# Scales for split weights: integer steps on VectorE in place of a maximum and a power on GpSimd

## The chip, the cores and the metric

The kernel runs on one core of a Trainium2 chip. The core has TensorE (PE in the profile), which multiplies matrices, VectorE (DVE), ScalarE (ACT), GpSimd (POOL), and SyncE (SP), which here only issues transfers. The engines run side by side, each with a queue of its own that it works off in order, and wait for one another through semaphores. The metric is the device time of one execution in microseconds (us). In the profile, times are counted from the first instruction, so its span is a little shorter than the execution.

## The reference

One encoder layer over 1024 tokens with 1024 features, in float32:

```python
hn = rmsnorm(x, norm_mix);  proj = hn @ w_in
o_a = window_gqa_sink(...)            # 8 heads, window 128, learned sink
o_b = neighbourhood_attention(...)    # 8 heads on the 16 x 64 grid
mix = concat([rmsnorm(o_a, norm_a), rmsnorm(o_b, norm_b)])
h = x + mix @ w_out
hn = rmsnorm(h, norm_ffn)
g, u = hn @ w_gate, hn @ w_up         # 2816 hidden columns
g = depthwise_conv3(g) + conv_b
h = h + (silu(g) * u) @ w_down
out = rmsnorm(h, norm_final)
```

## The kernel before, in words

**Products in parts.** Most float32 operands of PE are split: a high part (the value rounded to float16) and a low part (the rest). A product is then three matmuls, high by high, high by low and low by high. For float16 the operand is first brought to a good size by a scale that is a power of two, which is taken out again behind the product. ACT makes the high part (`activation` with `scale=`), DVE the low part (`scalar_tensor_tensor`: source times scale, minus the high part). In the feed-forward part this is `split_w` (L1140 and L1141) and `two_parts` (L1061 and L1062).

**Where a scale comes from.** For each block of 128 hidden columns ("unit"), ACT squares the block of `w_gate` and of `w_up` and sums each row (`head_scan`, L1054, for the first four units; `scan_rows`, L1154, for the others). The row sums stand in `head_rows` and `w_rows`. `settle_scales` takes them for up to four units at once. It adds the sums of gate and up (`wv`, L1021, on POOL) and calls `measure`. It then takes the reciprocal `back` (L1024, DVE), multiplies it by a common factor (L1025, POOL) and scales the three taps of the convolution of each unit by it (L1028, POOL).

**`measure`**, called with high priority, is a chain of steps on a tile of 128 by n numbers, n from 1 to 4:

- `spread_max`: PE transposes each column to all partitions (`wm`, L1001), DVE takes the maximum (L1003);
- L1010, POOL: the maximum with 1e-24, times 2^-26;
- L1011, POOL: the power -1/2;
- `exponent` (L240), DVE: a bit mask that keeps the exponent only, so that the scale is a power of two.

It runs ten times. Seven runs are from `settle_scales`: two with n = 2 in the second half of the output projection, four with n = 4 and one with n = 2 in the feed-forward part (`Weights.load`, L1277, for every fourth unit). Three are from `joint`, with n = 1: for `w_down` (L1598), and twice for the gated product (L1602 and L1715).

**The order of the work.** The input projection and the two attentions are interleaved. The output projection follows in two halves: `OutA` for the first four row blocks of `mix`, and the loop at L1233 to L1259 for the last four. This loop runs over two halves of the tokens (h) and eight output blocks (d). For each pair, PE runs 12 matmuls (L179) into a bank `pj`; DVE adds the result to `h1` (`settle_out`, L1188); ACT squares it (L1192), and the squares are summed on POOL for h = 0 (L1194) and on DVE for h = 1. `load_wo` splits the next block of `w_out` (ACT L1088, DVE L1089). Beside that the loop prepares the weights of the first four units: `settle_scales` at (h, d) = (0, 1) and (0, 3), `pure` and `head_weights` (ACT L1061, DVE L1062, and sums and differences of blocks, POOL L1209 and DVE L1201). When h = 0 is done, `inverse_power` gives the root mean square of the half: PE transposes (L220), DVE sums (L222, L223), POOL takes a power (L224). `widen` (PE, L255, tile `sw`) spreads it over the partitions, and DVE normalises `h1` with it (L1199).

The feed-forward part replaces eight block products of a 2 by 2 blocked product by seven (`p1` to `p7`, and `PRODUCTS` for the way down), with more sums and differences of blocks on DVE. A unit's results go to DRAM (`keep`) and come back as operands of the product with `w_down` (tile `dn`, `x_load`, `x_split`).

**What sets the order in the queues.** PE's instructions keep the order of the program (`manual_schedule`, L126). On the other engines the framework sorts the instructions when the program is built, by readiness and by priority: the place in the program, moved ahead inside a `high_priority` block. An instruction can thus run long before the program's place for it: the L1021 of the second group of feed-forward units ran at 472.31 us, its maximum (L1003) at 561.87 us. Buffers (14 tiles of the kind `op`, three `raw`, four each of `wv` and `m`) limit how far ahead that goes.

Of the kernel before, what the change touches and what calls it, by code (L numbers as in the profile page):

```python
# [16 lines left out]
I32 = mybir.dt.int32  # L17
AF = mybir.ActivationFunctionType
ALU = mybir.AluOpType
# [36 lines left out]
C_END = 128  # L56
V_TOP, P_TOP, TINY = 2.0 ** 14, 2.0 ** 15, 1e-30
X_TOP, W_TOP, FAINT = 2.0 ** 7, 2.0 ** 13, 1e-24

K_ID, K_MA, K_MB, K_SCALE, K_END = 0, 128, 512, 896, 897  # L60


def hybrid_layer(tc, xT, w_in, w_out, w_gate, w_up, w_down, small, sink, rpb, consts, rope, out):
    nc = tc.nc
    with ExitStack() as ctx:
# [25 lines left out]
        def bank(name, tag):  # L91
            return psum.tile([128, HALF], F32, name=name, tag=tag)
# [13 lines left out]
        minus_half = cpool.tile([128, 4], F32, name="minus_half")  # L106
# [109 lines left out]
        def inverse_power(sq, dim, tag):  # L216

            ps = bank("st", tag)
            for c in range(4):
                nc.tensor.transpose(ps[:, c * 128:(c + 1) * 128], sq[:, c * 128:(c + 1) * 128], ident)  # L220
            v = cpool.tile([128, 4], F32, name="v4", tag="v4", bufs=4)
            nc.vector.tensor_reduce(v, ps[:, :].rearrange("p (c w) -> p c w", w=128), axis=mybir.AxisListType.X, op=ALU.add)  # L222
            nc.vector.tensor_scalar(v, v, 1.0 / dim, EPS, op0=ALU.mult, op1=ALU.add)  # L223
            nc.gpsimd.tensor_tensor(v, v, minus_half, op=ALU.pow)  # L224
            return v

        def inverse_narrow(sqs, dim, tag, n=4):

            ps = bank("ss", tag)
            for i, sq in enumerate(sqs):  # L230
                for c in range(n):
                    nc.tensor.matmul(ps[:, c:c + 1], sq[:, c * 128:(c + 1) * 128], ones[:, 0:1], start=c == 0 and i == 0,
                                     stop=i == len(sqs) - 1, skip_group_check=True)
            v = cpool.tile([128, 4], F32, name="v4", tag="v4", bufs=4)
            nc.scalar.activation(v[:, 0:n], ps[:, 0:n], AF.Sqrt, bias=eps, scale=float(D) / dim)
            nc.vector.reciprocal(v[:, 0:n], v[:, 0:n])
            return v

        def exponent(x):
            nc.vector.tensor_scalar(x.bitcast(I32), x.bitcast(I32), 0x7F800000, None, op0=ALU.bitwise_and)  # L240
# [745 lines left out]
        def little(n, name, tag, bufs):  # L986

            if littles[1]:
                return littles[1].tile([128, n], F32, name=name, tag=tag, bufs=bufs)
            littles[0] += n  # L990
            return cst[:, littles[0] - n:littles[0]]

        def small(name, n=1):
            return little(n, name, name, 6)

        def spread_max(v, tag):

            n = v.shape[1]
            ps = bank("wm", tag)
            for i in range(n):  # L1000
                nc.tensor.transpose(ps[:, 128 * i:128 * i + 128], v[:, i:i + 1].to_broadcast([128, 128]), ident)  # L1001
            m = small("m", 4)[:, 0:n]
            nc.vector.tensor_reduce(m, ps[:, 0:128 * n].rearrange("p (c w) -> p c w", w=128), axis=mybir.AxisListType.X, op=ALU.max)  # L1003
            return m

        def measure(v, tag):

            with tc.high_priority(offset=500):
                s = spread_max(v, tag)
                nc.gpsimd.tensor_scalar(s, s, FAINT, W_TOP ** -2, op0=ALU.max, op1=ALU.mult)  # L1010
                nc.gpsimd.tensor_tensor(s, s, minus_half[:, 0:s.shape[1]], op=ALU.pow)  # L1011
                exponent(s)
            return s

        def settle_scales(i, n, tag):

            fs = FO[i:i + n]
            n = len(fs)
            rows = (w_rows if i >= HEAD else head_rows)[:, 2 * i:2 * i + 2 * n].rearrange("p (n s) -> p n s", s=2)
            v = small("wv", 4)[:, 0:n]  # L1020
            nc.gpsimd.tensor_tensor(v, rows[:, :, 0], rows[:, :, 1], op=ALU.add)  # L1021
            s = measure(v, tag)
            back = little(4, "back", "backs", 4)[:, 0:n]
            nc.vector.reciprocal(back, s)  # L1024
            nc.gpsimd.tensor_tensor(back, back, unit_back.to_broadcast([128, n]), op=ALU.mult)  # L1025
            for j, f in enumerate(fs):
                taps = little(3, "taps", "taps", 12)
                nc.gpsimd.tensor_scalar(taps, par[:, C_CW + 3 * f:C_CW + 3 * f + 3], back[:, j:j + 1], 1.0, op0=ALU.mult, op1=ALU.mult)  # L1028
                scale_of[f], back_of[f], taps_of[f] = s[:, j:j + 1], back[:, j:j + 1], taps
# [79 lines left out]
        for h in range(2):  # L1109
            wide = widen(vb2[h], "pt")  # L1110
            for i in range(4):
                x = mix[4 + i][:, tsl(h)]
# [120 lines left out]
        for h in range(2):  # L1233
            for d in range(KT):
                if h == 0 and d + 2 < KT:
                    wo.append(load_wo(d + 2, fpool))
                ps = bank("pj", ("o", "s", "pj")[(h * KT + d) % 3])
                for _ in product16(ps, wo[d], mg[4:8], h):
                    pass
                late.append((d, h, ps))  # L1240
                if h == 1 and d == 1:
                    with tc.high_priority(offset=300):
                        v = inverse_power(total[0], D, "pt")
                settle_out()
                if (h, d) in SETTLE_AT:
                    settle_scales(SETTLE_AT[h, d], 2, "pt")
                for f in PURE_AT.get((h, d), ()):
                    pure(FO[f])
                for when, name in ((S1_AT, "s1"), (S2_AT, "s2"), (S4_AT, "s4")):
                    for i, x in enumerate(when):  # L1250
                        if x == (h, d):
                            head_weights(i, name)
                if h == 1 and d == 2:
                    wide = widen(v, "pt")
                    normed(0, wide, K1)
                    B[1, 1] = operands([at(k, 0) for k in K1], "mix", "mix")
                if h == 1 and d == 4:
                    normed(0, wide, K2)
                    B[2, 1] = operands([at(k, 0) for k in K2], "mix", "mix")  # L1259
# [3 lines left out]
        class Weights:  # L1263
# [10 lines left out]
            def load(self):  # L1274
                i = FO.index(self.f)
                if i % 4 == 0:
                    settle_scales(i, 4, self.tag)  # L1277
                self.g, self.u = load_raw(w_gate[self.f], KT), load_raw(w_up[self.f], KT)
# [126 lines left out]
        def joint(rows):  # L1405
            with tc.high_priority(offset=500):
                v = small("v")
                nc.vector.tensor_reduce(v, rows, axis=mybir.AxisListType.X, op=ALU.max)
                return measure(v, "pt")
# [28 lines left out]
        with tc.high_priority(offset=300):  # L1438
            v = inverse_power(total[1], D, "pt")
# [262 lines left out]
        for i, (p, j, c) in enumerate(order):  # L1702
# [32 lines left out]
            if p == 6 and (j, c) == (0, 2):  # L1735
                for d in APART:
                    scaled(d, 1)
                vs[1] = inverse_narrow([sq[1]], D, "s")
# [5 lines left out]
        for k, cols in enumerate(quarters):  # L1744
            for j in (2, 3):
                ps = banks[6, j]
                for c, (f, n) in enumerate(PARTS):
                    group(ps[:, cols], dws[6, j, c], [[y[:, cols] for y in xs[6, f + q]] for q in range(n)], False, c == 2)
                    if todo:
                        todo.pop(0)()  # L1750
                    if (k, j, c) == (0, 3, 0):
                        for d in APART:
                            scaled(d, 0)
                    if (k, j, c) == (1, 2, 0):
                        vs[0] = inverse_narrow([parts[0, 2], parts[0, 3]], D, "s", 2)
                    if (k, j, c) == (1, 2, 1):
                        finish(0, vs[0], quarters[0])
                leave_quarter(j, ps, cols)
        first = quarters[1].start
        finish(0, inverse_narrow([parts[first, 2], parts[first, 3]], D, "s", 2), quarters[1], True)  # L1760


# [93 lines left out]
```

## Time and profile before

| what | us |
|---|---|
| median of 3 runs (range) | 1054.0 (1052.48 to 1055.39) |
| profiled execution | 1052.08 |
| its span, first to last instruction | 1050.3 |
| PE busy in the span | 1012.7 |
| DVE busy | 886.0 |
| ACT busy | 677.2 |
| POOL busy | 247.2 |
| L1003, start of the first and of the last of the ten | 378.6 and 850.3 |

"Busy" is the time in which an engine executes something; overlapping instructions count once. A line such as "PE sw L255 <- POOL v L224: 2.4, 1, 2.4" in the view of waits says that PE's instruction of L255 on tile `sw` waited for POOL's instruction of L224 on tile `v`: in total, how often, and the longest. In the view by time a line gives the start, the time to the end of the group, the engine, the line of the kernel and the instruction, with the tile written and the tiles read; the brackets at its end tell how long the engine stood still before it and whose work ended that. In the view by stage each engine has its busy time and its number of instructions, followed by the mean clock that PE was granted (1.00 is full speed), the share of the transfer engines and GB/s.

### The profile page before, as it was taken

The page shows a single profiled execution, that of the slowest core. Times are in us where ns is not written, and L with a number is a line of the kernel's source. Part 1 is how long each engine was busy: PE and PEld are TensorE (multiplying, and loading weights), DVE is VectorE, ACT ScalarE, POOL GpSimd, SP SyncE. Part 2 cuts the span into 40 slices and gives each one's busy share as a digit, 9 for nine tenths or more (in the row PEclk, how much of TensorE's full clock was granted, in tenths as well). Part 3 has the DMA queues.
Part 4 walks back from the last instruction along what each step waited for, and adds up shares of the span by engine and source line. Part 5 has one row for each costly group of instructions (what it writes and reads, how often), then busy time and mean ns, then how long its engine had stood idle before and what let it go on. Part 6 is the DMA issues. An engine that isn't in the chain of part 4 may idle for free.

```text
span 1050.3 us, 15578 instructions
## 1 busy us (share of the span) xinstructions
PE 1012.7 (96%) x5026; PEld 572.2 (54%) x5026; DVE 886.0 (84%) x1720; ACT 677.2 (64%) x1243; POOL 247.2 (24%) x379
## 2 busy tenths in 40 slices
PE   9998999999999977999999999999999999999996
PEld 7776777777775533444444444444444444444446
DVE  7699998766898789999899888888888889999874
ACT  8467787768687575778687875345454657655551
POOL 2235454676875344100101001001000000000002
PEclk9999999999999998999999999999999999999998
DMA  9437574686699743654767763332333678878744
GB/s 349 146 94 150 109 141 89 143 168 132 136 184 227 255 177 120 221 175 146 251 228 249 253 228 104 111 110 101 111 109 122 207 255 305 303 251 269 248 147 161
DMA packets 144274, 191.26 MB, mean 182 GB/s; under 512 B 77376, under 2 KB 88640, under 8 KB 144192
## 3 DMA queue, kind: packets, MB, share of 16 engines
q1 hardware_dynamic: 133536, 164.51, 54.9%
q10 hardware_dynamic: 10656, 25.76, 6.4%
q8 instruction: 39, 0.64, 0.3%
q14 instruction: 43, 0.35, 0.1%
HBM read 132.81 MB, written 28.57 MB: 154 GB/s over the span
## 4 chain that ended last, share of the span: by engine, by line
PE 60%; DVE 10%; ACT 4%; DMA 3%; issue 2%; POOL 1%; ACTq 0%; DVEq 0%; POOLq 0%
PE dn L1167 6%; PE dn L1165 6%; PE dn L1166 6%; PE z L1166 4%; PE z L1167 4%; PE z L1165 4%; PE pj L179 3%; PE y L1165 3%; PE y L1167 3%; PE y L1166 3%; PE x L1165 3%; PE x L1167 3%; PE x L1166 3%; PE pj L171 2%; PE pj L173 2%
## 5 line engine op out<-in xcount | busy, mean ns | idle before, releaser
L1167 PEld LDWEIGHTS <-wlo 128*128 128x128 f16 x898 | 87.8, 98 | 101.5 <-DVE wlo L1141 0.4
L1166 PEld LDWEIGHTS <-whi 128*128 128x128 f16 x898 | 87.8, 98 | 101.2 <-issue 0.9
L1165 PEld LDWEIGHTS <-whi 128*128 128x128 f16 x898 | 88.0, 98 | 100.2
L1167 PE MATMUL dn<-xd,wlo 128*128 128x512 f16 (+1 forms) x330 | 120.4, 365 | 0.0
L1166 PE MATMUL dn<-xd,whi 128*128 128x512 f16 (+1 forms) x330 | 120.4, 365 | 0.0
L1165 PE MATMUL dn<-xd,whi 128*128 128x512 f16 (+1 forms) x330 | 120.4, 365 | 0.0
L171 PE MATMUL pj<-xgh,whi 128*128 128x512 f32 x248 | 107.3, 433 | 0.6 <-ACT whi L155 0.6
L1167 PE MATMUL z<-hg,wlo 128*128 128x512 f16 x264 | 100.1, 379 | 0.0
L1165 PE MATMUL z<-hg,whi 128*128 128x512 f16 x264 | 100.1, 379 | 0.0
L1166 PE MATMUL z<-hg,whi 128*128 128x512 f16 x264 | 100.1, 379 | 0.0
L173 PE MATMUL pj<-xgh,wlo 128*128 128x512 f32 x248 | 98.3, 396 | 1.4 <-POOL wlo L156 1.4
L458 ACT ACTIVATE p<-p,nm 128x385 f32<-128x385 f32 (+3 forms) x128 | 74.7, 584 | 38.5 <-DVE nm L454 33.8
L172 PE MATMUL pj<-xgl,whi 128*128 128x512 f32 x248 | 97.9, 395 | 0.0
L1140 ACT ACTIVATE whi<-ws,m 128x512 f16<-128x512 f32 (+1 forms) x96 | 65.6, 708 | 33.2 <-DVE ws L1288 25.4
L1141 DVE SCALAR_TENSOR_TENSOR wlo<-ws,m,whi 128x512 f16<-128x512 f32 (+1 forms) x96 | 70.1, 739 | 13.2 <-ACT whi L1140 13.1
L1154 ACT ACTIVATE scan<-scan 128x1024 f32<-128x1024 f32 (+1 forms) x60 | 61.1, 1018 | 22.3 <-DMA scan<-in_w_down_dram 12.5
L1010 POOL TENSOR_SCALAR m<-m 128x4 f32<-128x4 f32 (+2 forms) x10 | 4.0, 404 | 256.1 <-DVE m L1003 255.9
L1141 DVE SCALAR_TENSOR_TENSOR wlo<-raw,m,whi 128x512 f16<-128x512 f32 (+1 forms) x78 | 55.1, 731 | 7.4 <-ACT whi L1140 6.7
L1165 PE MATMUL y<-hg,whi 128*128 128x512 f16 x160 | 60.6, 379 | 0.7 <-DVE c L1336 0.7
L1167 PE MATMUL y<-hg,wlo 128*128 128x512 f16 x160 | 60.6, 379 | 0.0
L1166 PE MATMUL y<-hg,whi 128*128 128x512 f16 x160 | 60.6, 379 | 0.0
L1140 ACT ACTIVATE whi<-raw,m 128x512 f16<-128x512 f32 (+1 forms) x78 | 51.5, 699 | 12.0 <-DMA raw<-in_w_down_dram 10.6
(290 smaller groups left out, 2490.1 us busy)
## 6 DMA issues: line engine op xcount, KB each, us to landing
xd<-x SPq DMA_DIRECT2D x77, 256.0 KB, 5.0
raw<-in_w_down_dram SPq DMA_DIRECT2D x64, 256.0 KB, 3.9
x<-c ACTq DMA_DIRECT2D x22, 512.0 KB, 2.9
scan<-in_w_gate_dram SPq DMA_DIRECT2D x18, 512.0 KB, 3.6
scan<-in_w_up_dram SPq DMA_DIRECT2D x18, 512.0 KB, 4.5
raw<-in_w_gate_dram SPq DMA_DIRECT2D x18, 512.0 KB, 3.5
raw<-in_w_up_dram SPq DMA_DIRECT2D x18, 512.0 KB, 3.8
raw<-in_w_in_dram SPq DMA_DIRECT2D x32, 256.0 KB, 3.2
```

The lines of the kernel that those rows point to most:

```text
L171: nc.tensor.matmul(ps, w[0], x[0][:, tsl(h)], start=first, stop=False)
L172: nc.tensor.matmul(ps, w[0], x[1][:, tsl(h)], start=False, stop=False)
L173: nc.tensor.matmul(ps, w[1], x[0][:, tsl(h)], start=False, stop=last)
L179: nc.tensor.matmul(ps, a, b, start=i == 0 and b is x[h][0] and a is w[0], stop=i == len(ws) - 1 and a is w[1])
L458: nc.scalar.activation(p[:, 0:e], p[:, 0:e], AF.Exp, bias=nm, scale=-1.0, accum_out=sm)
L1010: nc.gpsimd.tensor_scalar(s, s, FAINT, W_TOP ** -2, op0=ALU.max, op1=ALU.mult)
L1140: nc.scalar.activation(hi, src, AF.Copy, scale=by)
L1141: nc.vector.scalar_tensor_tensor(lo, src, by, hi, op0=ALU.mult, op1=ALU.subtract)
L1154: nc.scalar.activation(t, t, AF.Square, accum_out=dst)
L1165: nc.tensor.matmul(ps, w[0], x[0], start=first and i == 0, stop=False, skip_group_check=True)
L1166: nc.tensor.matmul(ps, w[0], x[1], start=False, stop=False, skip_group_check=True)
L1167: nc.tensor.matmul(ps, w[1], x[0], start=False, stop=last and i == len(ws) - 1, skip_group_check=True)
```

## The change

`measure` no longer uses POOL. Behind the maximum, `root_scale` runs three instructions on DVE, in place, on the bits of the maximum: shift right by one and mask; flip and mask; multiply by 2^76. The `exponent` step of `measure` is gone with the maximum and the power. The sum `wv` in `settle_scales` moves from POOL to DVE.

```diff
@@ -56,6 +56,7 @@
 X_TOP, W_TOP, FAINT = 2.0 ** 7, 2.0 ** 13, 1e-24
+W_ROOT = W_TOP * 2.0 ** 63
@@ -235,6 +236,13 @@
+        def root_scale(x):
+
+            i = x.bitcast(I32)
+            nc.vector.tensor_scalar(i, i, 1, 0x3FC00000, op0=ALU.logical_shift_right, op1=ALU.bitwise_and)
+            nc.vector.tensor_scalar(i, i, 0x3FC00000, 0x7F800000, op0=ALU.bitwise_xor, op1=ALU.bitwise_and)
+            nc.vector.tensor_scalar(x, x, W_ROOT, None, op0=ALU.mult)
@@ -1007,9 +1015,7 @@
                 s = spread_max(v, tag)
-                nc.gpsimd.tensor_scalar(s, s, FAINT, W_TOP ** -2, op0=ALU.max, op1=ALU.mult)
-                nc.gpsimd.tensor_tensor(s, s, minus_half[:, 0:s.shape[1]], op=ALU.pow)
-                exponent(s)
+                root_scale(s)
             return s
@@ -1018,7 +1024,7 @@
             v = small("wv", 4)[:, 0:n]
-            nc.gpsimd.tensor_tensor(v, rows[:, :, 0], rows[:, :, 1], op=ALU.add)
+            nc.vector.tensor_tensor(v, rows[:, :, 0], rows[:, :, 1], op=ALU.add)
             s = measure(v, tag)
```

How the bits give the scale: with E the eight exponent bits of the maximum m, the shift and the first mask leave half of E in the exponent's place, and the flip makes it 127 minus the whole part of E/2. As a float that is 2 to the power of minus that half; times 2^76 it is 2^(76 - floor(E/2)). Before, the scale was the power of two at or below 2^13 / sqrt(m). The two are equal where E is even. Where E is odd, the new one is twice the old one (equal if m is an exact power of four). Zero sums are no longer lifted to 1e-24; they give 2^76.

In `settle_scales`, the steps behind `measure` (L1024 to L1028) stay on their engines.

## The prediction

> **What bounds the kernel now.** I read the page's busy times first, then the busy time by stage, with stage borders at the places where the matrix engine (PE) stands still.
>
> ```profile
> PE 1012.7 (96%) x5026; PEld 572.2 (54%) x5026; DVE 886.0 (84%) x1720; ACT 677.2 (64%) x1243; POOL 247.2 (24%) x379
> ```
>
> ```profile
> 376.00:417.00 41.00, 30.27 (x125) 12.92 (x123) 36.73 (x48) 23.33 (x39) 24.28 (x23) 0.92 0.31 116
> 417.00:441.00 24.00, 23.98 (x115) 11.43 (x116) 23.18 (x38) 19.43 (x35) 1.43 (x2) 1.00 0.73 232
> 441.00:448.00 7.00, 4.89 (x17) 2.06 (x16) 5.14 (x9) 3.34 (x6) 2.46 (x1) 0.76 0.70 214
> 448.00:850.00 402.00, 400.81 (x1868) 182.78 (x1866) 351.65 (x508) 253.69 (x398) 19.64 (x42) 1.00 0.50 168
> ```
>
> In the stage rows the numbers are PE, weight loads, DVE, ACT, POOL, then the granted clock. All ten runs of `measure` lie between 376 and 852 us. Seven lie in the last row, where PE is busy 400.81 of 402 us: at most 1.2 us can be won there. One more follows at 850.3. The other two lie in the row 376 to 417, the second half of the output projection. There PE is idle 10.73 of 41 us and DVE is busy 36.73. What does PE wait for there, and what does DVE?
>
> ```profile
> PE pj L179 <- DVE wo L1089: 4.0, 2, 3.8
> PE sw L255 <- POOL v L224: 2.4, 1, 2.4
> PE st L220 <- POOL s L1194: 2.3, 1, 2.3
> PE pj L179 <- ACT wo L1088: 2.0, 2, 1.8
> ```
>
> ```profile
> DVE m L240 <- POOL m L1011: 2.8, 2, 2.1
> DVE h L1199 <- PE sw L255: 1.0, 1, 1.0
> DVE wo L1089 <- ACT wo L1088: 0.9, 1, 0.9
> ```
>
> PE's three longest waits end on DVE, or on POOL work that DVE feeds. DVE's longest wait is the one that the change removes: its mask L240 stands behind POOL's power L1011, 2.8 us in two waits. So this stage is DVE's, and what DVE saves in it moves its end, the `sw` transposes near 417 us. Behind them PE is busy 23.98 of 24 us, so a shift there travels to the end of the kernel. The stop in 441 to 448 hangs on the same work and shifts with it.
>
> **The change part by part.** DVE's queue around the first two measures, then POOL's (start, duration, instruction, and in brackets what was waited for):
>
> ```profile
> 378.59 0.41 DVE L1003 TENSOR_REDUCE m<-wm 128x2 f32<-128x256 f32 x1
> 379.93 0.75 DVE L1089 SCALAR_TENSOR_TENSOR wo<-wr,wo_by,wo 128x512 f16<-128x512 f32 x1 [0.92 <-ACT wo L1088]
> 381.28 1.24 DVE L240 TENSOR_SCALAR m<-m 128x2 int32<-128x2 int32 x1 [0.60 <-POOL m L1011]
> 382.44 2.07 DVE L1089 SCALAR_TENSOR_TENSOR wo<-wr,wo_by,wo 128x512 f16<-128x512 f32 x3
> ...
> 387.13 0.41 DVE L1003 TENSOR_REDUCE m<-wm 128x2 f32<-128x256 f32 x1
> ...
> 390.53 1.26 DVE L240 TENSOR_SCALAR m<-m 128x2 int32<-128x2 int32 x1 [2.15 <-POOL m L1011]
> 391.70 1.83 DVE L1062 SCALAR_TENSOR_TENSOR wp<-rw,m,wp 128x512 f16<-128x512 f32 x1
> 393.45 0.15 DVE L1024 RECIPROCAL back<-m 128x2 f32<-128x2 f32 x1
> 393.53 0.72 DVE L1188 SCALAR_TENSOR_TENSOR h<-pj,wo_back,h 128x512 f32<-128x512 f32 x1
> ...
> 394.84 1.40 DVE L1089 SCALAR_TENSOR_TENSOR wo<-raw,wo_by,wo 128x512 f16<-128x512 f32 x2
> ```
>
> ```profile
> 379.64 0.26 POOL L1010 TENSOR_SCALAR m<-m 128x2 f32<-128x2 f32 x1
> 379.99 1.26 POOL L1011 TENSOR_TENSOR m<-m,minus_half 128x2 f32<-128x2 f32 x1
> 381.23 1.27 POOL L1194 TENSOR_TENSOR s<-s,s 128x512 f32<-128x512 f32 x1
> ...
> 387.93 0.55 POOL L1010 TENSOR_SCALAR m<-m 128x2 f32<-128x2 f32 x1
> 388.55 1.28 POOL L1209 TENSOR_TENSOR ws<-rw 128x512 f32<-128x512 f32 x1
> 389.79 0.70 POOL L1011 TENSOR_TENSOR m<-m,minus_half 128x2 f32<-128x2 f32 x1
> 390.47 1.29 POOL L1209 TENSOR_TENSOR ws<-rw 128x512 f32<-128x512 f32 x1
> 391.73 1.25 POOL L1194 TENSOR_TENSOR s<-s,s 128x512 f32<-128x512 f32 x1
> ```
>
> *What three DVE steps cost.* The trace has a chain of two small DVE steps on one tile, the second an integer mask:
>
> ```profile
> 204.78 0.14 DVE L866 TENSOR_SCALAR ogm<-ogm 128x1 f32<-128x1 f32 x1
> 204.96 0.15 DVE L240 TENSOR_SCALAR ogm<-ogm 128x1 int32<-128x1 int32 x1
> ```
>
> From start to start they take 0.18 us, so I price the three at 0.54 us. A shift is in no row; as a `tensor_scalar` of the same size I give it the same price. The same mask can cost much more: 1.24 us at 381.28 and 1.26 us at 390.53, and both times it ends with the POOL instruction that runs beside it (381.23 + 1.27 = 382.50; 390.47 + 1.29 = 391.76). A small DVE step can thus be held for the whole of a POOL instruction. That is one exposed step per measure now and three after the change.
>
> *First measure, 378.59.* Gone are the wait of 0.60 and the mask's 1.16 (381.28 to 382.44), 1.76 us of DVE. The three steps fit into the 0.92 us that DVE waits for ACT ahead of 379.93, at a time when POOL, rid of L1010 and L1011, has nothing to run. What is late next is ACT's `wo` parts and POOL's sum L1194, which can start a little sooner than at 381.23, and beside which the next L1089 may be held. If it is held until that sum ends near 382.3, a start of 382.44 for the rest moves by little, and one L1089 (0.66 us) is done earlier: 0.7. If nothing holds it, I take 1.6 (the 1.76 less a sixth of a microsecond for ACT). I take **1.1**, the middle, since neither end has the nearer row.
>
> *Second measure, 387.13.* Gone are 2.15 of waiting and 1.17 (390.53 to 391.70), 3.32 us. In their place come 0.54 if POOL is idle; with one step held, 0.54 + 1.26 = 1.8; with all three held by one POOL instruction each, 3 x 1.28 = 3.84. POOL here runs one 1.3 us instruction after the other, so one hold is likely and gives a gain of **1.5**; the ends are 2.8 and -0.5. The low end also covers L1209 at 388.55, which ran while DVE was waiting anyway and may now hold a DVE split.
>
> *Adds moved to DVE (L1021).* L1024's 0.15 us with the next start 0.08 later bounds one from below; one chained step, 0.18, from above. Two in this stage: **-0.2** (ends -0.15 and -0.4, with some holding). The five others have cover: in 448 to 850 DVE is idle 50 of 402 us. Without that cover they cost 0.2 us each.
>
> *POOL* loses 2.77 us of scale work in this stage (0.26 + 1.26 + 0.55 + 0.70). Its sums and `ws` then come sooner, but they wait for ACT and DVE; I count nothing.
>
> *The eight later measures.*
>
> ```profile
> DVE m L240 <- POOL m L1011: 7.3, 8, 1.3
> ```
>
> ```profile
> PE y L1165 <- DVE c L1336: 0.7, 1, 0.7
> PE wm L1001 <- DVE v L1408: 0.5, 1, 0.5
> ```
>
> DVE waits 7.3 us less there, but PE's only two waits between 445 and 850 us are 0.7 and 0.5 us, the second for a reduce that stays. The scale of 850.3 is used by splits whose matmuls PE reaches later; PE's queue of matmuls is the cover throughout. I take 0 (ends 0 and 0.7); without the cover each measure would be worth about 0.6 (7.3 / 8 less two steps of 0.18). No DMA is issued, moved or removed. The new scale is the old one or twice it, and no duration depends on that.
>
> **Sum:** 1.1 + 1.5 - 0.2 = 2.4 us; ends 0.7 - 0.5 - 0.4 = -0.2 and 1.6 + 2.8 - 0.15 + 0.7 = 4.95. The profiled execution took 1052.08 us, 1.78 beyond its span, and the sum makes 1049.7 of it. It lay 1.9 under the median of 1054.0; against the median the same sum gives **1051.6**.
>
> **Rivals.**
>
> *The lock eats it.* All three steps of the second measure are held, and the L1089 of the first too. Then the gain is 0.7 - 0.5 - 0.2 = 0, so 1054. For it: both masks in this stage were held, and POOL is busy 24.28 of 41 us here. Against it: a hold needs POOL to start first each time, and at 391.70 to 393.53 DVE also ran L1062, L1024 and L1188 with only one visible hold. The Trainium skill, "SBUF — State Buffer", section "Who interferes with whom", says that DVE and POOL share one pair of ports as an exclusive lock, that a `tensor_scalar` in a two-port mode or an operation with two SBUF inputs can need it, and that whoever starts second blocks fully. By that rule, three steps in place of one are three chances to be blocked. The trace agrees as far as the two masks of 1.24 and 1.26 us go.
>
> *More than the sum.* PE's 3.77 us stop ahead of 395.63 goes entirely, and the spells of half clock with it:
>
> ```profile
> 395.63 11.79 PE L179 MATMUL pj<-mg,wo 128*128 128x512 f16 x46 [3.77 <-DVE wo L1089]
> ```
>
> ```profile
> 396.00:398.00 2.00, 2.00 (x7) 0.75 (x5) 2.00 (x3) 0.81 (x2) 2.00 (x2) 0.50 0.47 138
> ```
>
> After that stop the granted clock is 0.50. The spell here hides behind DVE; the one in 441 to 448 (mean 0.76 over 7 us, so 0.24 x 7 = 1.7 us) does not, since PE bounds what follows. If the stops fall so that it doesn't come, that is 1.7 on top of the upper 4.25 of this stage: 1054.0 - 5.95 = 1048. For it: the stop's cause, DVE's L1089 at 394.84 behind the second measure, is what the change removes. Against it: DVE's work until 417 stays as long as it is.
>
> *Slower: DVE waits for a scan.* POOL ran the sum L1021 as soon as ACT had the row sums, and sat idle until then at no cost:
>
> ```profile
> 437.54 1.26 POOL L1021 TENSOR_TENSOR wv<-w_rows 128x4 f32<-128x4 f32 x1 [20.58 <-ACT scan L1154]
> ```
>
> ```profile
> POOL wv L1021 <- ACT scan L1154: 117.4, 4, 30.3
> ```
>
> On DVE, whose queue is in order, the add must not stand ahead of its scan. If it stands before work that ran at 433 us, DVE waits about 4 us for 437.5, with the normalised halves and the second widen queued behind it, for which PE waits in 441 to 448. Price: 4 us, and the 1.7 us of half clock once more; with 2.4 gained, 1054.0 + 3.3 = 1057.3, and another 3 if a later group does the same. It decides from 2.4 us of waiting on. For it: ACT's scans wait for DMAs, so their place is uncertain. Against it: the sum isn't used until about 500 us, and DVE's other work there comes earlier in the program.
>
> **How the numbers follow.** Forecast 0.40 (its own range 1050 to 1053); the lock 0.20; more than the sum 0.22; slower 0.18. A measurement of this kernel can tell about 0.3%, 3.2 us, from no change: faster means under 1050.8. That is the case "more", 0.22, and two fifths of the forecast, 0.16, together 0.38. Slower, over 1057.2, is most of the last case and a tail of the lock, 0.18. The rest, 0.44, is within 0.3%. Leaving out about 0.1 on each side, the range goes from 1047 to 1058.
>
> **What would show it.** After: no wait of DVE for POOL at the two measures; three DVE steps behind each L1003, of 0.15 us each, or one or more near 1.3 us, ending with a POOL instruction (the lock). The `sw` transposes at 414 to 415 us in place of 417.02, and the same shift at 850. The stage's PE idle time near 8 us in place of 10.73. PE still over 99% busy from 448 to 850. The forecast is wrong if DVE waits for ACT's `scan` at the moved add, or if the shift at 417 is lost by 520, where PE waited 0.7 us.

## The result, and the profile after

| | median, us (range, runs) | ratio to the kernel before, 95% interval |
|---|---|---|
| before, first set | 1053.74 (1051.11 to 1056.46, 10) | |
| after, first set | 1050.73 (1049.13 to 1051.82, 10) | 0.9972 [0.996, 0.9984] |
| before, second set | 1052.57 (1049.84 to 1057.87, 31) | |
| after, second set | 1051.32 (1048.75 to 1055.59, 12) | 0.9994 [0.9976, 1.0011] |

The first set says 3.0 us faster, the second 1.25, with no change inside its interval. The intervals overlap from 0.9976 to 0.9984; over both sets the medians are 1051.0 (22 runs) against 1052.9 (41), 1.9 us apart. The forecast, 1051.6, lies 0.9 above the first median and 0.3 above the second. The profiled execution took 1051.22 us, its span is 1049.4.

The lines of the kernel after that answer to those of before: L240 is now L248, and the steps of `root_scale` are L243, L244 and L245; L1003 is L1011, L1021 is L1027, L1024 is L1030, L1062 is L1068, L1089 is L1095, L1188 is L1194, L1194 is L1200. First the page's busy times, then the view by stage.

```profile
PE 1010.0 (96%) x5026; PEld 569.8 (54%) x5026; DVE 889.6 (85%) x1747; ACT 677.4 (65%) x1243; POOL 229.8 (22%) x352
```

```profile
376.00:417.00 41.00, 31.00 (x131) 13.45 (x128) 37.90 (x54) 23.04 (x39) 20.07 (x18) 0.92 0.32 119
417.00:441.00 24.00, 22.89 (x110) 10.94 (x111) 22.93 (x38) 19.07 (x36) 1.05 (x1) 1.00 0.74 227
441.00:448.00 7.00, 4.82 (x25) 2.26 (x24) 5.39 (x10) 4.35 (x9) 2.64 (x1) 1.00 0.67 208
448.00:850.00 402.00, 401.33 (x1870) 183.10 (x1869) 355.09 (x530) 254.10 (x399) 7.19 (x24) 1.00 0.50 169
```

POOL is rid of its scale work (24.28 to 20.07 us in the first row, 19.64 to 7.19 in the last). But PE stands still for 10.00 us of the first stage, against 10.73 before: it won almost nothing there. (Near 396 us it waits 1.95 us for `wo` in place of 3.77, but at the stage's end 4.0 us for POOL's last sum in place of 2.3.) The clock of the third row is 1.00 where it was 0.76. What PE and DVE wait for in that stage:

```profile
PE st L221 <- POOL s L1200: 4.0, 1, 4.0
PE pj L180 <- DVE wo L1095: 2.6, 2, 1.9
PE pj L180 <- ACT wo L1094: 1.8, 1, 1.8
```

```profile
DVE wv L1027 <- ACT junk L1060: 1.7, 1, 1.7
DVE h L1194 <- PE pj L180: 1.3, 2, 0.7
```

The wait for POOL's power is gone. In its place DVE waits 1.7 us for ACT, at the moved add. DVE's queue around the two measures:

```profile
377.99 0.74 DVE L1194 SCALAR_TENSOR_TENSOR h<-pj,wo_back,h 128x512 f32<-128x512 f32 x1
380.46 0.16 DVE L1027 TENSOR_TENSOR wv<-head_rows 128x2 f32<-128x2 f32 x1 [1.73 <-ACT junk L1060]
380.54 0.75 DVE L1194 SCALAR_TENSOR_TENSOR h<-pj,wo_back,h 128x512 f32<-128x512 f32 x1
381.20 0.41 DVE L1011 TENSOR_REDUCE m<-wm 128x2 f32<-128x256 f32 x1
...
389.65 0.42 DVE L1011 TENSOR_REDUCE m<-wm 128x2 f32<-128x256 f32 x1
389.98 1.30 DVE L1068 SCALAR_TENSOR_TENSOR wp<-rw,m,wp 128x512 f16<-128x512 f32 x1
391.20 1.26 DVE L243 TENSOR_SCALAR m<-m 128x2 int32<-128x2 int32 x1
392.38 1.83 DVE L1068 SCALAR_TENSOR_TENSOR wp<-rw,m,wp 128x512 f16<-128x512 f32 x1
394.13 0.16 DVE L244 TENSOR_SCALAR m<-m 128x2 int32<-128x2 int32 x1
394.32 0.17 DVE L245 TENSOR_SCALAR m<-m 128x2 f32<-128x2 f32 x1
...
395.91 0.75 DVE L1095 SCALAR_TENSOR_TENSOR wo<-raw,wo_by,wo 128x512 f16<-128x512 f32 x1
```

Read it from three marks: the first `h` of L1194 (377.99; before 376.84), the second maximum (389.65; before 387.13) and the first `wo<-raw` (395.91; before 394.84). From the first mark to the second it takes 11.66 us against 10.29 before: 1.4 **lost**. From the second to the third it takes 6.26 against 7.71: 1.45 **won**, with one of the three steps held (1.26 us). Together they cancel.

**Where one profiled execution differs from the other.** PE's instructions have the same order in both kernels, so the start of one and the same instruction can be compared along the trace. In the profile after, PE is 1.08 us behind at 366 us. Up to there the code is the same, and over the other twelve profiles of this study this number lies between -1.6 and +1.1: it is noise. From 366 to 417 us nothing is added (1.09 at 417). Then 1.6 us are won at 444 to 447, where the profile before had a spell of half clock, and 0.8 at 512 to 519, where PE no longer waits for DVE's L1336. Behind 850 us 0.5 is lost. The sum is 0.9, the difference of the spans. In the second set's profile of after (span 1050.3, as long as before's) the spell near 444 is back; the other parts are the same: -0.1 in the stage, 0.8 at 519, 0.5 given back.

So the theory at this point was: the gain is the shorter stage (as forecast), partly hidden. The rivals: it comes from 519 us, or from the spells of half clock.

### The profile page after: what moved, and what is told of

The parts are those of the page before. It is cut to its first block, busy times and chain, and to the rows that moved or that the text cites. A ratio compares the mean times of both kernels' runs of the same rounds, so it can differ in the third digit from the quotient of the medians.

```text
span 1049.4 us, 15576 instructions
## 1 busy us (share of the span) xinstructions
PE 1010.0 (96%) x5026; PEld 569.8 (54%) x5026; DVE 889.6 (85%) x1747; ACT 677.4 (65%) x1243; POOL 229.8 (22%) x352
## 4 chain that ended last, share of the span: by engine, by line
PE 67%; DVE 9%; issue 1%; ACT 1%; DMA 1%; POOL 1%; ACTq 0%; DVEq 0%; POOLq 0%
PE dn L1173 6%; PE dn L1171 6%; PE dn L1172 6%; PE z L1172 5%; PE z L1173 5%; PE z L1171 5%; PE pj L180 4%; PE y L1172 4%; PE y L1173 4%; PE y L1171 4%; PE x L1172 3%; PE x L1173 3%; PE x L1171 3%; PE pj L172 2%; PE pj L174 2%; PE pj L173 2%
## 5 line engine op out<-in xcount | busy, mean ns | idle before, releaser
L1555 DVE SCALAR_TENSOR_TENSOR xd<-xd,m 128x512 f16<-128x512 f32 x77 | 55.2, 747 | 7.1 <-ACT xd L1554 7.1
```

The lines of the kernel that those rows point to most:

```text
L1555: nc.vector.scalar_tensor_tensor(lo, t[:, HALF:S], by, hi, op0=ALU.mult, op1=ALU.subtract)
```

## The experiments

**Which of the ten measures?** Three kernels keep the old steps for some of them; a fourth puts back one edit. The kernel before ran 34 times beside them: 1052.36 us (1050.12 to 1055.71).

```diff
-        def measure(v, tag):
+        def measure(v, tag, root=True):
...
-                root_scale(s)
+                if root:
+                    root_scale(s)
+                else:
+                    nc.gpsimd.tensor_scalar(s, s, FAINT, W_TOP ** -2, op0=ALU.max, op1=ALU.mult)
+                    nc.gpsimd.tensor_tensor(s, s, minus_half[:, 0:s.shape[1]], op=ALU.pow)
+                    exponent(s)
...
-            nc.vector.tensor_tensor(v, rows[:, :, 0], rows[:, :, 1], op=ALU.add)
-            s = measure(v, tag)
+            (nc.gpsimd if i >= HEAD else nc.vector).tensor_tensor(v, rows[:, :, 0], rows[:, :, 1], op=ALU.add)
+            s = measure(v, tag, i < HEAD)
...
-                return measure(v, "pt")
+                return measure(v, "pt", False)
```

This is `heads_only`; `ffn_only` has the conditions turned round, `first_ffn_only` has only `i == HEAD` new, and `head_adds_pool` has all ten measures new and only the add of `i < HEAD` on POOL.

> Only the two measures with n = 2 in the output projection are changed (their sums and their three steps on DVE); the eight later ones are as before. Theory of the prediction (the gain is made in 376 to 417 us): about 2.4 us faster than before, and the widen transposes of the first half, at 417.0 us in before, come 2 to 3 us sooner. Rival, from the two traces (the stage wins nothing, since the sum on DVE waits 1.7 us for ACT's last row sums of the head and the steps are held beside POOL's sums; the gain is made near 519 us): within 0.5 us of before, the widen transposes where they were, and the wait of PE y for DVE c near 519 us, 0.7 us in before, still there. Third theory (the gain is only the spell of half clock at 444 us, which the profile of after happens not to have): within 0.5 us in the median.

> The two measures of the output projection are as before; all eight later ones are changed. Theory of the prediction: no gain, at most 0.7 us. Rival (the gain is made near 519 us): the whole gain, 2 to 4 us faster than before, and no wait of PE y for DVE c near 519 us. Third theory (a spell of half clock at 444 us, by chance): within 0.5 us in the median, the spell present or absent as it falls.

> Only the measure at 500.9 us (n = 4, the first behind the four head units) and its sum are changed, the nine others are as before. Rival (the gain is made near 519 us, by what this one measure does to the queues of DVE and ACT): 2 to 4 us faster than before, like the whole change. Theory of the prediction and third theory: within 0.7 us of before.

> After, with the two sums of the output projection back on POOL, so that DVE no longer waits 1.73 us for ACT's row sums; everything else as in after. If this wait is what took the forecast gain of the stage, the widen transposes come 1 to 1.7 us sooner than in after (418.1 less the start of the stage), and the time is 1 to 1.7 us below after, about 4 to 4.7 below before. If the stage is bound by something else, such as POOL's sums of squares or the steps held beside POOL, the time is that of after, 3 us below before.

| kernel | median, us (range, runs) | ratio, 95% interval |
|---|---|---|
| heads_only | 1050.74 (1048.46 to 1052.15, 10) | 0.9981 [0.9971, 0.999] |
| ffn_only | 1052.43 (1048.88 to 1055.23, 11) | 0.9995 [0.9983, 1.0008] |
| first_ffn_only | 1051.9 (1050.2 to 1055.37, 12) | 0.9993 [0.9981, 1.0006] |
| head_adds_pool | 1051.32 (1048.06 to 1054.43, 12) | 0.9984 [0.9973, 0.9996] |

With the two measures of the output projection alone the median is 1.6 us lower; the eight later ones alone change nothing that these runs can tell. That speaks for the place that the prediction named. How much of the 1.6 us is the shorter stage is not shown: the runs of `heads_only` had a mean granted clock of 0.9929, those of the kernel before 0.9916. At 1.7 us a spell of half clock is 0.0016 of the mean, so the 0.0013 answers to some 1.4 us (an estimate). In its profile the `sw` transposes start at 415.56 us in place of 417.02, but 0.71 us of that was there at 366 us: the stage won 0.75 us, not the expected 2 to 3. `head_adds_pool` missed both cases of its expectation. It lies 1.0 us below the kernel before, not 4 to 4.7 and not 3. By the starts of PE's instructions its stage won 1.25 us, and 0.8 was lost again just ahead of 512 us (more on this below).

Inside the stage, the four kernels show separate prices. The add on DVE waits in `heads_only` just as in after, yet the first part takes 10.18 us there and not 11.66. The difference is PE's next run of 22 matmuls, first of after, then of `heads_only`:

```profile
382.33 6.61 PE L180 MATMUL pj<-mg,wo 128*128 128x512 f16 x22 [0.63 <-DVE wo L1095]
```

```profile
380.55 4.92 PE L180 MATMUL pj<-mg,wo 128*128 128x512 f16 x22 [0.63 <-DVE wo L1100]
```

The same work takes 1.7 us more, at half clock, and DVE's two waits of 0.6 to 0.7 for `pj` come from it. With the add on POOL (`head_adds_pool`) the first part takes 9.75 us. The spell is not the add's doing alone, though: `held_pool`, a later kernel with the add on POOL, has it too, and there the first part takes 11.22 us:

```profile
380.10 6.61 PE L180 MATMUL pj<-mg,wo 128*128 128x512 f16 x22 [0.18 <-DVE wo L1100]
```

So the add on DVE costs 0.4 us, without a spell (10.18 - 9.75) and with one (11.66 - 11.22; 11.67 in the repeat of after), and the spell costs 1.5 us wherever the add stands. The wait of 1.73 us costs so little since DVE waits 1.26 us in that stretch anyway when the add is on POOL (0.34 for `pj` and 0.92 for ACT's `wo` in the profile of `head_adds_pool`); 0.47 is left. On DVE the add makes PE's stop ahead of the 22 matmuls longer (0.63 us in place of 0.18); whether that makes a spell likelier was not measured.

In `head_adds_pool` one step of the first measure is held, and in this kernel and in `heads_only` two of the second; its rows:

```profile
381.40 0.16 DVE L243 TENSOR_SCALAR m<-m 128x2 int32<-128x2 int32 x1
381.47 0.75 DVE L1100 SCALAR_TENSOR_TENSOR wo<-wr,wo_by,wo 128x512 f16<-128x512 f32 x1
382.13 1.24 DVE L244 TENSOR_SCALAR m<-m 128x2 int32<-128x2 int32 x1
...
388.57 1.26 DVE L243 TENSOR_SCALAR m<-m 128x2 int32<-128x2 int32 x1
389.75 1.86 DVE L1073 SCALAR_TENSOR_TENSOR wp<-rw,m,wp 128x512 f16<-128x512 f32 x1
391.53 1.23 DVE L244 TENSOR_SCALAR m<-m 128x2 int32<-128x2 int32 x1
```

With two holds the second part takes 6.99 us in both kernels (gain 0.7), with one 6.26. One hold was seen only behind a spell in the first part (after, its repeat, `held_pool`), two where none came: the delay seems to move DVE's steps against POOL's work, and 0.6 to 0.8 us of the spell come back in this way. No run tests that by itself.

The rival "519" falls as the source of 2 to 4 us, but it has a part; apart from the spells it is the largest one in the two profiles of after. In every kernel with the new measure at 500.9 us, PE wins 0.8 between 512 and 519. (`held_before`, a later kernel with the old one, wins as much there: in its profile PE comes 1.6 us later to the place than in the kernel before, and does not wait.) Three of the kernels with the new measure lose time just before it, `ffn_only` 1.5, `head_adds_pool` 0.8 and `first_ffn_only` 0.7, so their medians don't price the place by itself. In `ffn_only` PE waits for a split that stands on ACT behind a scan, which waits for its transfer. Its view of waits from 498 to 522 us, and ACT's rows:

```profile
PE x L1176 <- ACT whi L1151: 1.0, 1, 1.0
PE x L1178 <- DVE wlo L1152: 0.2, 1, 0.2
```

```profile
507.61 1.06 ACT L1165 ACTIVATE scan<-scan 128x1024 f32<-128x1024 f32 x1 [1.36 <-DMA scan<-in_w_gate_dram]
...
508.67 1.32 ACT L1151 ACTIVATE whi<-raw,m 128x512 f16<-128x512 f32 x2
```

In after that split starts at 506.18 and PE does not wait.

**Spells of half clock, and how much there is to win.** Beside a repeat of after, two kernels put eight matmuls in front of each widening of an `h1` half, where PE stands still, and one kernel has a constant for the two scales. The kernel before: 1052.57 (31 runs).

```diff
-        def widen(v, tag, n=4):
+        def widen(v, tag, n=4, warm=None):
...
             wide = bank("sw", tag)
+            if warm:
+                for _ in range(8):
+                    nc.tensor.matmul(wide[:, :], warm[0], warm[1], start=True, stop=True)
```

```diff
+        def measure(v, tag, known=False):
...
+                if known:
+                    s = small("m", 4)[:, 0:v.shape[1]]
+                    nc.vector.memset(s, 2.0 ** 11)
+                    return s
```

> The changed kernel once more, on the chip of the three kernels beside it. If the gain is the shorter stage of 376 to 417 us, the median is 2 to 3 us below the kernel before and the granted clock, mean over the runs, is the same within 0.0005. If the gain is fewer spells of half clock, the mean clock is higher by 0.001 to 0.002 (one spell of 3.4 us at 0.5 is 1.7 us, or 0.0016 of the mean). Under both, the time from the first settle_out of the stage to the second wo of raw is 17 to 18 us in its profile, against 18.0 before.

> The kernel before, with eight extra matmuls of 128x512 in front of each of the two widenings of the h1 halves (near 417 and 444 us), where PE otherwise stands still for about 2 us; they write into a bank that the widening overwrites. If spells of half clock behind those stops take part in the difference, none lies between 412 and 450 us any more and the median is 1.0 to 1.7 us below the kernel before, less what the extra matmuls themselves delay (0 to 1). If the spells have no part in it, the median stays within 0.5 us of the kernel before or lies above it.

> The changed kernel with the same extra matmuls. Shorter stage: 2 to 3 us below the kernel before with those matmuls, as the changed kernel is below the one before without them. Fewer spells: less than 1 us between the two, since neither has a spell there.

> The changed kernel with a constant scale in place of the two measures of the output projection: their transposes, maxima and scale steps are left out, the row sums and the splits stay. It bounds what a cheaper measure can win there. If DVE's queue bounds the stage, as the prediction says, it goes further below the changed kernel by about what is left of the two measures on DVE (two maxima and six steps, 1.9 to 4 us), so 4 to 7 us below the kernel before. If something else bounds the stage (ACT's parts, or POOL's sums), it is within 1 us of the changed kernel.

| kernel | median, us (range, runs) | ratio, 95% interval |
|---|---|---|
| after_again | 1051.32 (1048.75 to 1055.59, 12) | 0.9994 [0.9976, 1.0011] |
| warm_before | 1053.73 (1051.27 to 1057.8, 12) | 1.0016 [0.9999, 1.0033] |
| warm_after | 1053.63 (1051.15 to 1058.98, 12) | 1.0014 [0.9998, 1.0031] |
| known_heads | 1048.69 (1046.92 to 1051.54, 8) | 0.9965 [0.9949, 0.9981] |

`after_again` came out below its expectation (1.25 us, not 2 to 3), at a mean granted clock of 0.9916 against 0.9912 for the kernel before: the 0.0004 answer to 0.4 us, a third of what sets the two medians apart. `known_heads` answers to the first of its two cases only by half: 3.9 us below the kernel before, at the low end of 4 to 7. A measure that costs nothing would win 3.9 (at a mean clock of 0.9923); the change wins a third of that in this set.

The two kernels with extra matmuls miss both theories. They lie 1.1 to 1.2 us above the kernel before, at the edge of their intervals, and 0.1 us apart. In the profile of `warm_before` the spells at 409 and 444 are gone (the first of the two without help, since the extra matmuls start at 412.21; `warm_after` has one of two steps from 409.27), and PE is 1.6 us further ahead at 500 us than at 366. But then it waits (view of waits, 498 to 522 us):

```profile
PE x L1168 <- ACT whi L1143: 2.4, 1, 2.4
PE x L1168 <- ACT c L1327: 0.6, 1, 0.6
PE x L1170 <- DVE wlo L1144: 0.2, 1, 0.2
```

It is the split of `ffn_only`; here it starts at 507.91 us, 1.1 later than in the kernel before, again behind a scan that waited for its transfer. So these two kernels don't say what the spells are worth. They show that time won ahead of 500 us can be lost at 508.

**What holds a step, and the order of the scans.** Three kernels in one set (the kernel before: 1052.57, 26 runs), then the edits together (the kernel before: 1052.64, 11 runs). `psum_pool` is `head_adds_pool` with the steps of the measures with two columns in PSUM; the one later measure with two columns is changed with them. In `held_before` and `held_pool` the scans follow the first split of the first settled unit; `psum_held_pool` has all of it.

```diff
+            x = ps[:, 128 * n:129 * n] if raw else m
-            nc.vector.tensor_reduce(m, ps[:, 0:128 * n].rearrange("p (c w) -> p c w", w=128), axis=mybir.AxisListType.X, op=ALU.max)
+            nc.vector.tensor_reduce(x, ps[:, 0:128 * n].rearrange("p (c w) -> p c w", w=128), axis=mybir.AxisListType.X, op=ALU.max)
...
+                if v.shape[1] == 2:
+                    x, s = spread_max(v, tag, True)
+                    i = x.bitcast(I32)
+                    nc.vector.tensor_scalar(i, i, 1, 0x3FC00000, op0=ALU.logical_shift_right, op1=ALU.bitwise_and)
+                    nc.vector.tensor_scalar(i, i, 0x3FC00000, 0x7F800000, op0=ALU.bitwise_xor, op1=ALU.bitwise_and)
+                    nc.vector.tensor_scalar(s, x, W_ROOT, None, op0=ALU.mult)
...
```

```diff
-            nc.scalar.activation(hi, src, AF.Copy, scale=by)
+            done = nc.scalar.activation(hi, src, AF.Copy, scale=by)
...
+            if FO[HEAD] in scale_of:
+                mark.setdefault("first", done)
...
-            nc.scalar.activation(t, t, AF.Square, accum_out=dst)
+            with behind(*["first"] * ("first" in mark)):
+                nc.scalar.activation(t, t, AF.Square, accum_out=dst)
```

> The changed kernel with the two head sums back on POOL, and with the maximum and the first two scale steps of the two measures of the output projection kept in PSUM beside the transposes; the third step brings the scale to SBUF. Theory: a small DVE step is held by a running POOL instruction only where both its sides are in SBUF. Then the steps take 0.15 to 0.3 us each, and from the second maximum to the first wo of raw it takes 4.6 to 5.2 us in place of 6.99; the median is 1 to 2 us below the kernel with the two sums on POOL alone (1051.32), so about 1049.5. Rival: DVE waits for POOL whatever it reads; then one or two steps are still near 1.25 us and that distance stays near 7.

> The kernel before, with the row scans of later units (L1154) put behind the first split of the first settled unit in ACT's queue, so that this split (the whi near 507 us) no longer stands behind scans that wait for their transfers. Nothing is left out. Theory: part of what is won ahead of 500 us is lost near 508, where PE waits for this split. In the profile of the kernel before PE did not wait there, so its own time moves little: 0 to 1.5 us lower in the median, by the runs in which it did wait. Rival: the place is of no account; the median stays within 0.5 us, or rises by what the scans are late for later.

> The changed kernel with the two head sums back on POOL and the same order of the scans. If the loss near 508 us is what keeps the gain small, PE does not wait there for the split, and the median lies 2 to 3 us below the kernel before with that order (1.2 to 2 from the stage up to 412 us, 0.8 near 519). If not, the difference is the 1.0 to 1.4 us that was found without the new order.

> The changed kernel with all three edits at once: the two head sums on POOL, the first two scale steps of the two measures of the output projection in PSUM, the row scans of later units behind the first split. If the order of the scans adds its gain to that of the steps in PSUM, the median lies 4.5 to 5.5 us below the kernel before, so near 1047.5. If both win the same time at the place near 508 to 519 us, it lies where the kernel without the new order of scans lies, 3.8 us below, near 1048.8.

| kernel | median, us (range, runs) | ratio, 95% interval |
|---|---|---|
| psum_pool | 1048.77 (1046.72 to 1050.49, 9) | 0.996 [0.9946, 0.9975] |
| held_before | 1050.42 (1049.66 to 1053.37, 12) | 0.9979 [0.9966, 0.9991] |
| held_pool | 1050.06 (1047.27 to 1053.96, 12) | 0.9978 [0.9963, 0.9993] |
| psum_held_pool | 1047.7 (1046.69 to 1050.02, 6) | 0.9956 [0.994, 0.9972] |

The second measure of `psum_pool` on DVE, and what POOL ran beside it:

```profile
387.18 0.42 DVE L1012 TENSOR_REDUCE wm<-wm 128x2 f32<-128x256 f32 x1
387.51 1.42 DVE L1081 SCALAR_TENSOR_TENSOR wp<-rw,m,wp 128x512 f16<-128x512 f32 x1
388.85 0.15 DVE L1021 TENSOR_SCALAR wm<-wm 128x2 int32<-128x2 int32 x1
388.92 1.72 DVE L1081 SCALAR_TENSOR_TENSOR wp<-rw,m,wp 128x512 f16<-128x512 f32 x1
390.55 0.15 DVE L1022 TENSOR_SCALAR wm<-wm 128x2 int32<-128x2 int32 x1
390.74 0.16 DVE L1023 TENSOR_SCALAR m<-wm 128x2 f32<-128x2 f32 x1
...
392.23 1.41 DVE L1108 SCALAR_TENSOR_TENSOR wo<-raw,wo_by,wo 128x512 f16<-128x512 f32 x2
```

```profile
387.08 2.99 POOL L1228 TENSOR_TENSOR ws<-rw 128x512 f32<-128x512 f32 x2
390.05 1.71 POOL L1213 TENSOR_TENSOR s<-s,s 128x512 f32<-128x512 f32 x1
```

POOL is busy without a break from 387.08 to 391.76, and all three steps take 0.15 to 0.16 us. From the second maximum to `wo<-raw` it takes 5.05 us, inside the expected 4.6 to 5.2. The theory of the hold stands: a small step can be held where it reads and writes SBUF, and none was held that read from PSUM. The Trainium skill, "SBUF — State Buffer", section "Who interferes with whom", has it so that the lock concerns DVE's second pair of ports to SBUF; the rows agree (1.25 us in SBUF, 0.15 in PSUM, under the same POOL work). What is left to hold are the splits with two SBUF inputs (1.42 and 1.72 us in place of 0.7).

The order of the scans helps the kernel before by 2.15 us, more than expected; in its profile PE waits for nothing from 498 to 522 us. The other expectation was missed: `held_pool` lies 0.4 us below `held_before`, not 2 to 3. By these medians the change is worth little once the scans are out of the way; but the two intervals are 2.6 and 3.2 us wide, so a gain of 1 to 2 us is not ruled out. All edits together are the fastest kernel of the study, 4.9 us below the kernel before (from the first `h` to `wo<-raw` it takes 14.2 us in its profile, against 18.0 before); from `psum_pool` it differs by 1.1 us, which 9 and 6 runs in different sets do not settle.

## Why the prediction was right, and where not

The number was right, in part by luck. The stage named was the right one to look at, but in the two profiles of after it won 0.0 and 0.1 us, not 2.4, and 0.8 came from 519 us, for which the sum had 0. Of the two large terms one was met.

- **What bounds the kernel: right.** What DVE saves in the stage from 376 to 417 us can reach the end: with constants the kernel wins 3.9 us, with unheld steps 3.8. With the two measures alone it wins 1.6, of which its profile places 0.75 in the stage.
- **Second measure, 1.5 with one hold: right, with luck.** 1.45 was won with one step held, but only behind a spell of half clock; without one it was 0.7 with two held. With none held it was 2.7 and 3.1 (7.71 less 5.05 in `psum_pool`, 4.59 in `psum_held_pool`); the forecast's ends were -0.5 and 2.8.
- **First measure, 1.1 (ends 0.7 and 1.6): the sizes were off.** Without the add, 0.5 was won (10.29 - 9.75), with one step held for 1.24 us behind POOL's sum. With no step held (`psum_held_pool`, 9.62) it was 0.7, the low end, since the next split then took 1.42 us, as the prediction had it there.
- **The adds, -0.2 (ends -0.15 and -0.4): the step that failed.** They were priced by how long an add takes. The first ran at 373.10 us, ahead of the stage, and waited for nothing. What counts for the second is what it waits for: 1.73 us for ACT's row sums, with the `settle_out` behind it in DVE's queue. On POOL that wait cost nothing; on DVE it cost 0.4 us, the low end for both. The third rival had just this mechanism, but looked for it at the later adds: the one at 439.15 us, for which it set 4 us, waited for nothing.
- **No term for a new spell.** The sum had nothing for a spell of half clock in the first part. In after it took 1.5 us there, of which 0.6 to 0.8 came back in the second part.
- **The eight later measures, 0 (0 to 0.7): near.** 0.8 was won at 519 us. DVE now runs L1342, the old L1336, at 514.96, ahead of three splits which stood before it at 516.81 to 518.80:

```profile
514.96 0.68 DVE L1342 TENSOR_TENSOR c<-y,c 128x512 f32<-128x512 f32 x1
515.56 1.41 DVE L1147 SCALAR_TENSOR_TENSOR wlo<-ws,m,whi 128x512 f16<-128x512 f32 x2
516.88 0.75 DVE L1147 SCALAR_TENSOR_TENSOR wlo<-raw,m,whi 128x512 f16<-128x512 f32 x1
```

  That is a new order of the queue, found when the program was built, more than the shorter measure itself.
- **What would show it.** No wait for POOL, a step near 1.3 us and PE over 99% busy from 448 to 850 (401.33 of 402) came as said. The `sw` transposes did not: they start at 418.11, 1.09 behind the old 417.02 and no earlier than the noise of the start makes them; nor did PE's idle time near 8 us (10.00). The prediction took a DVE wait for ACT's `scan` at the moved add for a sign that it is wrong; the wait came at the add for the first units, for their scan (`junk`).
- **The rivals.** The lock took one of three steps, as forecast. The spell near 444 us went in one profile of after and not in the other. "Slower" was right in kind, at another add and for 1.7 us.

**What stays open.** In the two profiles of after the parts behind 366 us sum up to 2.0 and 0.5 us won, most of the difference one spell; the medians say 3.0 and 1.25. Some 1 us of the medians is thus not placed. The runs of both kernels spread over 3 to 8 us, and much of that goes with the clock: of the 26 runs of the kernel before beside `psum_pool`, those at a mean granted clock of 0.989 took 1055.2 to 1056.9 us, those at 0.993 took 1049.0 to 1051.6. The kernels in which the stage is shortest ran at a higher clock than the kernel before beside them (0.9928 against 0.9912 for `psum_pool`). Whether a shorter stage brings fewer spells, or the runs were lucky, is open. Why `held_pool` wins so little over `held_before` was not tried further.

## What to carry to other kernels

Before a step moves to another engine, read what it waits for, and not only how long it takes: on an idle engine a wait is free; in a full queue that is worked off in order everything behind it pays what the queue would not have waited anyway. A small step on DVE beside a busy POOL is best put where POOL does not hold it; here that was PSUM, worth 2.5 us over the same kernel with its steps in SBUF (1051.32 to 1048.77, in two sets; the profiles place 1.9 of it at the second measure). Where an effect is smaller than the spread of the runs, repeat the whole comparison, and compare the granted clocks, before you explain its size.

## What the runs showed of the hardware

Spells of half clock lie on a raster. In the profile before they start at 61.48, 395.99, 409.64 and 443.78 us, each a whole multiple of 3.413 us after the other; over the 14 profiles they last one step of the raster or two, apart from the one at the kernel's end. Cut into windows on that raster, from 340 to 515 us of these profiles, every window at full clock in which PE was busy for up to 0.41 of the time was followed by a spell (34 windows), and none in which it was busy for 0.43 or more. The border is not sharp: near 58 us, elsewhere in the program, a window with PE busy for 0.43 (after) and one with 0.47 (its repeat) were followed by a spell too. So a stop of the same length may cost nothing or 1.7 us, by where the raster falls. The second widening stops PE for 2.1 to 2.2 us in both kernels. Before, then after, in windows on the raster of each (busy times as in the view by stage):

```profile
440.37:443.78 3.41, 1.30 (x7) 0.56 (x6) 2.23 (x5) 2.17 (x6) 2.64 (x1) 1.00 0.67 222
443.78:447.19 3.41, 3.41 (x11) 1.40 (x10) 2.73 (x5) 1.63 (x3) 0.00 (x0) 0.50 0.69 184
```

```profile
440.96:444.37 3.41, 1.54 (x8) 0.48 (x5) 2.80 (x6) 2.29 (x5) 2.38 (x1) 1.00 0.68 232
444.37:447.79 3.42, 3.11 (x17) 1.68 (x18) 2.42 (x4) 2.06 (x4) 0.26 (x1) 1.00 0.68 193
```

1.30 of 3.41 us (0.38) brings the spell, 1.54 (0.45) does not. The raster lies otherwise against the program in each profile, so part of the spread of the runs is luck of this kind. The Trainium skill, "TensorE: Matmul & The Clock Gate", section "What's actually happening", describes such a window of 3413 ns that does not start with the kernel; the spells here agree. The Trainium skill, "TensorE: Matmul & The Clock Gate", section "Why this matters for your kernels", warns of gaps above about 3 us; here a stop of 2.1 us was enough, and the measurement decides.
